# First convolution block's low weight parts by VectorE, S2 formed second, head 0's cached keys requested as attention opens, merge steps later

## The chip, the cores and the metric

The kernel runs on one core of one Trainium2 chip. Its time is the device time of one execution in microseconds (us), as the median of several runs. TensorE (PE) multiplies, VectorE (DVE), ScalarE (ACT) and GpSimd (POOL) do the element-wise work, and the queue of SyncE (SP) issues most of the transfers; POOL issues those that accumulate. Each engine takes its instructions in the order in which the program emits them.

## What is computed

One inference step of a decoder trunk with four layers, for 512 prompt tokens and 8 sample tokens that share every weight. The token mixers are an mLSTM matrix memory (layer 0), a gated short convolution (1), a dilated windowed attention (2) and a causal pooling (3); each layer ends with a gated per-layer embedding. What the change touches, cut from the reference:

```python
x += mixer(rms_norm(x, norm_g[i]))
x = x + sigmoid(x @ pg_w[i]) * (p[i] @ pe_w[i])

# layer 1
bg, cg, xb, z = split(h @ w_in, 4)            # w_in is the kernel's w_b
cx = cg * xb
y = conv_w[0] * cpad[:, 0:T] + conv_w[1] * cpad[:, 1:1+T] + conv_w[2] * cpad[:, 2:2+T]
out = (bg * y * silu(z)) @ w_out

# layer 2, three dilation groups per head: softmax statistics of each group, then
mx = max over groups of m
num = sum over groups of l * exp(m - mx) * o ;  den = sum of l * exp(m - mx)
```

For the sample tokens the keys and values of attention come from a cache (`kc0` to `kc2`, `vc0` to `vc2`).

## The kernel before

**Products.** All matrices are float32. Each weight tile (128x1024, 512 KB) and each activation is split into a high part and a low part in the reduced format fp32r, and a product is three matmuls: high by high, high by low, low by high (`mm6`, L334 to L338). A projection over 1024 inputs is 48 matmuls on 256 or 264 columns. Its sum lies in one of two PSUM buffers (`ps`), which is drained by DVE or ACT into an `a` tile before the projection after the next may begin.

**Weights.** `plan` lists the weight tiles in the order of use, one `Item` for a single tile and one for a pair. `due` gives each step on an item a planned time: load (SP, L270), high part (ACT, L253), low part. The low part is DVE's subtraction weight minus high part (L262), or, for items marked `moved`, ACT writes minus the high part (L258) and POOL issues a transfer that adds the weight onto it (L260). Before, all tiles of `w_b` and `w_bo` are moved; of a pair only the first. `pump` emits the steps that are due whenever PE's program has moved on. There are four buffers each of loaded weights (`wf`) and of high and low parts (`wh`, `wl`).

**Convolution layer.** The first three channel blocks (`NPLAIN`) are four single projections each, with the tiles 32+j, 16+j, j, 48+j of `w_b`. The norm of the layer's input runs beside the first block: PE adds the squares (L533), ACT takes the root (L534), DVE the reciprocal (L536), and only then can the first projections be drained, by a multiplication with that reciprocal (L485). After that the norm's generator `summed` forms sums of the activations on POOL (L582 to L585) and splits them on ACT and DVE (L589 to L602). From block 3 on, two tiles at a time go through `seven`, a Strassen-like form with seven products of 12 matmuls each: `r1` collects products 1 and 4, and ACT copies `r1` (L377) between them. It needs sums of the two tiles, made by POOL in the step `sum` (S1, the difference in place of the second tile, S2, S4: L277 to L280), then split by ACT into `hs` and by DVE into `ls` at the times given in `due`. The last product of a pair is kept back (`pend`) and emitted after the fourth product of the next pair (`flush`), followed by what the block does with its result (L1109, L1071, L1076 to L1079).

**Streams.** Between the projections' matmuls generators are advanced: one tick after every second `mm6`, so four ticks in a projection. In the mLSTM and in attention `main` (the prompt's work of a head) takes one step a tick; in attention `samp` (the sample tokens' work) takes 1.15. A `yield` ends a step. Head `hd`'s generators start when its projections are done, and so run beside those of head `hd+1`.

**mLSTM head.** `mlstm_head` scales `num` on DVE (L961), yields four times, and has PE transpose it (L967).

**Attention head.** `attn_head` adds the masks (L1238 to L1259), reduces and exponentiates (L1233), bounces the statistics through memory (L1251, L1252), takes the maximum over groups and subtracts it (L1276 to L1278, DVE), exponentiates that (L1279, ACT), scales the probabilities (L1281 to L1292, DVE), waits six steps and transposes them (L1300, PE). `attn_sample_steps` waits two steps, has PE transpose the queries (L1390), sends them to memory (L1393), fetches them back broadcast (`qb`, L1364) and the cached keys (`kc`, L1366), waits six steps and takes dot products on DVE (`sum_k`, L459). At attention's opening SP loads the rotary tables (L1162) and the mask (L1164).

Of the kernel before, what the change touches and what calls it, by code (L numbers as in the profile page):

```python
# [8 lines left out]
F32 = mybir.dt.float32  # L9
# [5 lines left out]
P = 128  # L15
NP = 512
NS = 8
# [25 lines left out]
MOVED = ("w_b", "w_bo")  # L43


class Item:


    def __init__(self, *keys, cost=5.76, life=None):
        self.keys, self.cost, self.life = keys, cost, life  # L50
        self.moved = keys[0][0] in MOVED


def paired(j):
# [58 lines left out]
def due(items):  # L113

    ops, t, seq = [], 0.0, 0
    slots = {"wf": [0.0] * FBUFS, "wh": [0.0] * HBUFS, "hs": [0.0] * SBUFS}

    def take(tag, until):
        free = slots[tag]
        at = min(free)  # L120
        free.remove(at)
        free.append(until)
        return at

    def at(time, i, op):
        nonlocal seq
        ops.append((time, seq, i, op))
        seq += 1
        return time

    for i, it in enumerate(items):
        it.begin = t
        if len(it.keys) == 1:
            ld = min(slots["wf"])
            sp = at(max(ld, take("wh", t + (it.life or it.cost))), i, "split")
            at(take("wf", sp + 3) - 0.01, i, "load")
        else:
            ld, ld2 = sorted(slots["wf"])[:2]
            one = at(max(ld, ld2, t - 12.8), i, "sum")
            h1 = at(max(ld, take("wh", t + 5.76), t - 14.4), i, "high")  # L140
            h2 = at(max(ld2, take("wh", t + 10.08), one + 6.6), i, "high2")
            low1 = at(h1 + 1.3 if it.moved else max(h1 + 1.3, one + 3), i, "low")
            low2 = at(max(h2 + 1.3, one + 3), i, "low2")
            at(take("wf", max(low1, one + 7) + 1) - 0.01, i, "load")
            at(take("wf", low2 + 3) - 0.01, i, "load2")
            for n, need, until in (("2", t - 4.6, t + 2.88), ("1", t - 3.4, t + 4.32), ("4", t - 1.4, t + 17.3)):
                h = at(max(take("hs", until), need, one + 3), i, "high" + "s" + n)
                at(h + 0.6, i, "lows" + n)
        t += it.cost
    return sorted(ops)  # L150
# [42 lines left out]
class Net:  # L193
# [47 lines left out]
    def make(self, i, op):  # L241

        if (i, op) in self.made:
            return
        self.made.add((i, op))
        nc, it = self.nc, self.items[i]
        t = self.wt.setdefault(i, {})
        f = lambda tile: tile.bitcast(F32)
        new = lambda tag, n=1024, pool=None, dt=F32R: (pool or self.wp).tile([P, n], dt, tag=tag, name=self.nm(tag))

        def high(k, tag, n=1024, pool=None):
            t["h" + k] = new(tag, n, pool)
            nc.scalar.activation(t["h" + k], t["w" + k], AF.Copy)  # L253

        def low(k, tag, n=1024, pool=None):
            t["l" + k] = new(tag, n, pool)
            if k == "1" and it.moved:
                nc.scalar.activation(t["l1"], f(t["h1"]), AF.Copy, scale=-1.0)  # L258
                key = it.keys[0]
                nc.gpsimd.dma_start(t["l1"], self.d[key[0]][key[1:]], accum_op=ALU.add)  # L260
                return
            nc.vector.tensor_sub(t["l" + k], t["w" + k], f(t["h" + k]))  # L262

        a, b = slice(0, 512), slice(512, 1024)
        sub = nc.gpsimd.tensor_sub
        if op in ("load", "load2"):
            n = 2 if op == "load2" else 1
            key = it.keys[n - 1]
            t[f"w{n}"] = self.wp.tile([P, 1024], F32, tag="wf", name=self.nm("wf"), bufs=FBUFS)
            nc.sync.dma_start(t[f"w{n}"], self.d[key[0]][key[1:]])  # L270
        elif op == "split":
            high("1", "wh")
            low("1", "wl")
        elif op == "sum":
            w1, w2 = t["w1"], t["w2"]
            s1, s2, s4 = (self.act()[:, :512] for _ in range(3))
            nc.gpsimd.tensor_add(s1, w2[:, a], w2[:, b])  # L277
            sub(w2[:, a], w1[:, a], w2[:, a])
            sub(s2, s1, w1[:, a])
            sub(s4, w1[:, b], s2)  # L280
            t.update(ws1=s1, ws2=s2, ws4=s4)
        else:
            k = op.removeprefix("high").removeprefix("low") or "1"
            step = high if op.startswith("high") else low
            if k[0] == "s":
                step(k, op[0] + "s", 512, self.sp)
            else:
                step(k, "w" + op[0])
# [590 lines left out]
    def mlstm_head(self, hd, q, k, v, so, rows, S):  # L879
        nc, d, m2 = self.nc, self.d, S["m2"]  # L880
# [78 lines left out]
        nc.vector.reciprocal(ss, ss)  # L959
        nc.vector.tensor_mul(ri, ri, ss)  # L960
        nc.vector.tensor_mul(num[:, :, :256], num[:, :, :256], ri.unsqueeze(2).broadcast_to([P, 4, 256]))  # L961
        for _ in range(4):
            yield
        for u in range(2):
            hp = self.aux()
# [186 lines left out]
    def attention(self, h, lay):  # L1152
        nc, d, tc = self.nc, self.d, self.tc
        rope, main, samp = Stream(1), Stream(1), Stream(1.15)
        self.streams = [self.norm, rope, main, samp, self.gate]
        o, self.o_done = [], []
        with ExitStack() as st:
            mp = lay.enter_context(tc.tile_pool(name="at", bufs=1))
            m2 = lay.enter_context(tc.tile_pool(name="at2", bufs=2))
            cs = [self.act()[:32] for _ in range(4)]  # L1160
            for i in range(4):
                nc.sync.dma_start(cs[i], d["rope"][:, i])  # L1162
            mask = mp.tile([P, 512], F32, name="mask")
            nc.sync.dma_start(mask, d["mask"])  # L1164
            for hd in range(H):
                q, k, v = [], [], []
                for g in range(3):
                    keep = 0 if g else NP - P
                    out, tab = (self.by_residue, cs[2:]) if g else (self.scaled, cs[:2])
                    q.append(out(self.proj("w_c", 24 * g + hd, a=h)))  # L1170
                    rope.gens.append(self.rope(q[g], tab))
                    k.append(out(self.proj("w_c", 24 * g + 8 + hd, a=h)))
                    rope.gens.append(self.rope(k[g], tab, d[f"o_k{g}"][hd], keep))
                    v.append(out(self.proj("w_c", 24 * g + 16 + hd, a=h)))
                    nc.sync.dma_start(d[f"o_v{g}"][hd], v[g][:, keep:T])
                rope.drain()
                o.append(self.act())
                main.gens.append(self.attn_head(q, k, v, o[hd], m2, mask))
                samp.gens.append(self.attn_sample(hd, q, k, v, o[hd], m2))
            y, zs = [], []  # L1180

            sent = []

            def gate():
                while len(sent) < min(len(zs), len(self.o_done)):
                    n = len(sent)
                    sent.append(n)
                    self.gated(y, zs[n], o[n], False)

            for j in range(H):  # L1190
                zs.append(self.scaled(self.proj("w_c", 72 + j, a=h)))
                if j > 1:
                    gate()

        def finish():
            main.drain()
            samp.drain()
            gate()

        self.finish = finish  # L1200
        return y
# [13 lines left out]
    def attn_head(self, q, k, v, o, m2, mask):  # L1215
        nc = self.nc
# [47 lines left out]
        for g in range(3):  # L1264
# [3 lines left out]
            t = self.act()  # L1268
# [7 lines left out]
        nc.vector.tensor_max(ma, m3[:, 0], m3[:, 1])  # L1276
        nc.vector.tensor_max(ma, ma, m3[:, 2])
        nc.vector.tensor_sub(m3, m3, ma.unsqueeze(1).broadcast_to([P, 3, 4]))  # L1278
        nc.scalar.activation(mx, mx, AF.Exp)  # L1279
        yield  # L1280
        nc.vector.tensor_mul(l, l, mx)  # L1281
# [3 lines left out]
        f = m2.tile([P, 12], F32, tag="f", name=self.nm("f"))  # L1285
# [41 lines left out]
        for n, i in enumerate(order):  # L1327
            g, c, cols = uses[i]
# [3 lines left out]
        nc.vector.tensor_copy(o[:, :NP], op)  # L1332
        yield

    def attn_sample(self, hd, q, k, v, o, m2):
        nc, d = self.nc, self.d
        mm = nc.tensor.matmul
        qs = m2.tile([P, 3, NS], F32, tag="qs", name=self.nm("qs"))
# [2 lines left out]
        for g in range(3):  # L1341
# [5 lines left out]
            nc.gpsimd.tensor_copy(two(qs[:, g]), new(q[g]))  # L1347
            nc.gpsimd.tensor_mul(two(qk[:, g]), new(q[g]), new(k[g]))
            nc.gpsimd.tensor_copy(two(vn[:, :, g]), new(v[g]))
        return self.attn_sample_steps(hd, qs, qk, vn, o, m2)  # L1350

    def attn_sample_steps(self, hd, qs, qk, vn, o, m2):
        nc, d = self.nc, self.d
        mm = nc.tensor.matmul
        off = (0, 128, 256)
        wait = lambda n: range(n)
# [4 lines left out]
        def load_k(g):  # L1361
            n = NROWS[g]
            qb.append(m2.tile([P, NS, P], F32, tag="qb", name=self.nm("qb")))
            nc.sync.dma_start(qb[g][:n], scr[g].partition_broadcast(n))  # L1364
            kc.append(m2.tile([P, NS, P], F32, tag="kc", name=self.nm("kc")))
            nc.sync.dma_start(kc[g][:n], d[f"kc{g}"][hd])  # L1366

# [17 lines left out]
                if b % 4 == 3:  # L1385
                    yield

        yield from wait(2)
        qp = self.aux()
        nc.tensor.transpose(qp[:24, :P], qs.rearrange("p a b -> p (a b)"), self.ident)  # L1390
        qt = m2.tile([24, P], F32, tag="qt", name=self.nm("qt"))
# [287 lines left out]
```

## Time and profile before

| | us |
|---|---|
| median of 3 runs | 2178.26 |
| lowest and highest | 2176.53, 2182.1 |
| the profiled execution, its own time | 2174.19 |
| its span in the trace | 2172.4 |

| engine | busy us | share of the span |
|---|---|---|
| PE | 2134.1 | 98% |
| DVE | 1393.8 | 64% |
| ACT | 901.0 | 41% |
| POOL | 415.1 | 19% |

The span is what the trace shows of the program; the execution's own time has 1.8 us more around it. An engine's "idle before" is the time it stood still just ahead of an instruction, and the name behind the arrow is what ended that wait. PEclk is TensorE's granted clock, 1.00 for 2.4 GHz and 0.50 for 1.2 GHz.

### The profile page before, as it was taken

The page shows a single profiled execution, that of the slowest core. Times are in us where ns is not written, and L with a number is a line of the kernel's source. Part 1 is how long each engine was busy: PE and PEld are TensorE (multiplying, and loading weights), DVE is VectorE, ACT ScalarE, POOL GpSimd, SP SyncE. Part 2 cuts the span into 40 slices and gives each one's busy share as a digit, 9 for nine tenths or more (in the row PEclk, how much of TensorE's full clock was granted, in tenths as well). Part 3 has the DMA queues.
Part 4 walks back from the last instruction along what each step waited for, and adds up shares of the span by engine and source line. Part 5 has one row for each costly group of instructions (what it writes and reads, how often), then busy time and mean ns, then how long its engine had stood idle before and what let it go on. Part 6 is the DMA issues. An engine that isn't in the chain of part 4 may idle for free.

```text
span 2172.4 us, 42676 instructions
## 1 busy us (share of the span) xinstructions
PE 2134.1 (98%) x17560; PEld 2112.8 (97%) x17560; DVE 1393.8 (64%) x3060; ACT 901.0 (41%) x1438; POOL 415.1 (19%) x491
## 2 busy tenths in 40 slices
PE   8999999999999999999999999999999999999998
PEld 8999999999999999999998999999999999999998
DVE  7676667653466766751477787787876566676434
ACT  6444454432465554554333333333335342322233
POOL 1101110100035545521014332232320000000000
PEclk9999999999999999999999999999999999999999
DMA  5644454332277666687233555455555233223421
GB/s 165 207 159 139 155 183 159 99 106 90 86 170 165 156 175 156 154 200 184 88 118 121 191 174 178 158 190 167 184 165 185 88 113 101 88 90 96 127 79 50
DMA packets 113527, 307.32 MB, mean 141 GB/s; under 512 B 34324, under 2 KB 38676, under 8 KB 111284
## 3 DMA queue, kind: packets, MB, share of 16 engines
q1 hardware_dynamic: 104404, 272.54, 38.2%
q0 software_dynamic: 8784, 31.99, 8.5%
q8 instruction: 138, 2.26, 0.4%
q14 instruction: 57, 0.47, 0.1%
q10 hardware_dynamic: 144, 0.06, 0.0%
HBM read 281.72 MB, written 22.82 MB: 140 GB/s over the span
## 4 chain that ended last, share of the span: by engine, by line
PE 80%; DVE 9%; issue 3%; ACT 3%; DMA 3%; POOL 1%; SPq 0%; DVEq 0%; ACTq 0%; POOLq 0%
PE ps L334 21%; PE ps L336 21%; PE ps L338 21%; PE ax L364 1%; DVE wl L262 1%; PE ax L362 1%; PE ax L363 1%; PE ax L334 1%; PE ax L338 1%; PE ax L336 1%; PE ps L362 1%; PE ps L363 1%; PE ps L364 1%; PE ax L1329 1%; DMA kc<-kc 1%
## 5 line engine op out<-in xcount | busy, mean ns | idle before, releaser
L334 PE MATMUL ps<-hi,wh 128*128 128x256 f32 x4672 | 964.0, 288 | 11.1 <-DVE a L485 7.1
L336 PE MATMUL ps<-lo,wh 128*128 128x256 f32 x4672 | 941.7, 283 | 1.0 <-DVE lo L800 0.8
L338 PE MATMUL ps<-hi,wl 128*128 128x256 f32 x4672 | 941.5, 283 | 0.6 <-DMA wl<-w_bo 0.4
L334 PEld LDWEIGHTS ps<-hi,wh 128*128 128x128 f32 x4672 | 727.2, 189 | 17.7 <-issue 7.4
L336 PEld LDWEIGHTS ps<-lo,wh 128*128 128x128 f32 x4672 | 725.9, 189 | 1.4 <-DVE lo L800 1.0
L338 PEld LDWEIGHTS ps<-hi,wl 128*128 128x128 f32 x4672 | 725.5, 189 | 1.0 <-DMA wl<-w_bo 0.6
L262 DVE TENSOR_TENSOR wl<-wf,wh 128x1024 fp32r<-128x1024 f32 x283 | 356.6, 1263 | 179.0 <-ACT wh L253 176.5
L253 ACT ACTIVATE wh<-wf 128x1024 fp32r<-128x1024 f32 x344 | 361.0, 1053 | 162.2 <-issue 86.3
L1207 POOL TENSOR_TENSOR a<-a,a 32x520 f32<-32x520 f32 x48 | 74.4, 1551 | 273.5 <-DVE a L485 101.8
L502 ACT ACTIVATE a<-ps 128x520 f32<-128x520 f32 x42 | 47.6, 1133 | 133.4 <-PE ps L338 112.2
L260 POOL DMA_DIRECT2D wl<-w_b x45 | 39.8, 884 | 327.4 <-ACT wl L258 308.1
L627 DVE TENSOR_TENSOR x<-ps,x 128x520 f32<-128x520 f32 x32 | 22.4, 699 | 122.8 <-PE ps L338 122.7
L1208 POOL TENSOR_TENSOR a<-a,a 32x520 f32<-32x520 f32 x48 | 66.3, 1382 | 144.6 <-DVE a L1206 98.5
L489 ACT ACTIVATE a<-a 128x520 f32<-128x520 f32 x42 | 26.8, 639 | 147.2 <-DVE a L485 147.1
L466 ACT ACTIVATE hi<-x 128x520 fp32r<-128x520 f32 x32 | 20.5, 639 | 156.9 <-DVE x L627 156.9
L485 DVE TENSOR_TENSOR a<-ps,a 128x520 f32<-128x520 f32 x85 | 59.0, 694 | 21.2 <-PE ps L338 17.8
L649 DVE TENSOR_TENSOR a<-ax,a 128x256 f32<-128x256 f32 (+1 forms) x62 | 23.7, 424 | 75.3 <-ACT a L647 75.3
L459 DVE CUSTOM_DVE_ANT_0 kc<-kc,qb 128x128 f32<-128x128 f32 (+1 forms) x192 | 58.0, 356 | 20.7 <-DMA kc<-kc 20.7
L1233 ACT ACTIVATE S<-S,nmx 128x128 f32<-128x128 f32 (+1 forms) x96 | 39.9, 417 | 72.3 <-DVE nmx L1230 72.3
L258 ACT ACTIVATE wl<-wh 128x1024 fp32r<-128x1024 f32 x61 | 64.6, 1058 | 1.6
L459 DVE CUSTOM_DVE_ANT_0 vc<-vc,pb 128x128 f32<-128x128 f32 (+1 forms) x192 | 61.8, 379 | 1.8 <-DMA pb<-scr_p 1.3
L262 DVE TENSOR_TENSOR ls<-a,hs 128x512 fp32r<-128x512 f32 x57 | 62.6, 1128 | 0.0
(344 smaller groups left out, 2890.5 us busy)
## 6 DMA issues: line engine op xcount, KB each, us to landing
wf<-w_c SPq DMA_DIRECT2D x80, 512.0 KB, 5.6
wf<-w_a SPq DMA_DIRECT2D x64, 512.0 KB, 3.7
wf<-w_b SPq DMA_DIRECT2D x64, 512.0 KB, 3.6
wl<-w_b POOLq DMA_DIRECT2D x45, 512.0 KB, 6.4
wf<-w_pg SPq DMA_DIRECT2D x32, 512.0 KB, 3.6
wf<-w_d SPq DMA_DIRECT2D x32, 512.0 KB, 3.4
pb<-scr_p SPq DMA_DIRECT2D x8, 1292.0 KB, 6.5
Ci<-C_in SPq DMA_DIRECT2D x16, 512.0 KB, 7.5
```

What stands on the lines that cost most here:

```text
L253: nc.scalar.activation(t["h" + k], t["w" + k], AF.Copy)
L258: nc.scalar.activation(t["l1"], f(t["h1"]), AF.Copy, scale=-1.0)
L262: nc.vector.tensor_sub(t["l" + k], t["w" + k], f(t["h" + k]))
L334: mm(out[j], wh, a[0][:, PARTS[j]], start=start, stop=False)
L336: mm(out[j], wh, a[1][:, PARTS[j]], start=False, stop=False)
L338: mm(out[j], wl, a[0][:, PARTS[j]], start=False, stop=stop)
L362: mm(out, w[0][:, c], hi, start=start and k == 0, stop=False, **go)
L459: self.nc.vector.tensor_tensor_reduce(junk, a, b, 1.0, 0.0, ALU.mult, ALU.add, out)
L485: nc.vector.tensor_mul(dst[:, :T], ps, self.r)
L502: nc.scalar.activation(dst, split(ps), AF.Copy)
L1207: nc.gpsimd.tensor_mul(b[:32], t[:32], cs[0])
L1208: nc.gpsimd.tensor_mul(a[:32], a[:32], cs[1])
```

## The change

Five edits. The tiles 0, 16, 32 and 48 of `w_b` (first block) are no longer moved, so DVE makes their low parts. In the pairs POOL forms S2 ahead of the difference that replaces the second tile, and the splits of S2, S1 and S4 are due 2.2, 1.4 and 0.6 us earlier. In mLSTM's head 0 the transposes come two ticks later. In attention the keys `kc0` and `kc1` of head 0 are requested at the opening, into the two buffers of that tag, and head 0's `samp` waits four steps instead of two. In every attention head one `yield` stands between L1278 and L1279.

```diff
-        self.moved = keys[0][0] in MOVED
+        name, j = keys[0][:2]
+        self.moved = name in MOVED and not (name == "w_b" and j % 16 == 0)
...
-            for n, need, until in (("2", t - 4.6, t + 2.88), ("1", t - 3.4, t + 4.32), ("4", t - 1.4, t + 17.3)):
+            for n, need, until in (("2", t - 6.8, t + 2.88), ("1", t - 4.8, t + 4.32), ("4", t - 2.0, t + 17.3)):
...
             nc.gpsimd.tensor_add(s1, w2[:, a], w2[:, b])
+            sub(s2, s1, w1[:, a])
             sub(w2[:, a], w1[:, a], w2[:, a])
-            sub(s2, s1, w1[:, a])
             sub(s4, w1[:, b], s2)
...
         nc.vector.tensor_mul(num[:, :, :256], num[:, :, :256], ri.unsqueeze(2).broadcast_to([P, 4, 256]))
-        for _ in range(4):
+        for _ in range(4 if hd else 6):
             yield
...
             nc.sync.dma_start(mask, d["mask"])
+            early = []
+            for g in range(2):
+                early.append(m2.tile([P, NS, P], F32, tag="kc", name=self.nm("kc")))
+                nc.sync.dma_start(early[g], d[f"kc{g}"][0])
...
         nc.vector.tensor_sub(m3, m3, ma.unsqueeze(1).broadcast_to([P, 3, 4]))
+        yield
         nc.scalar.activation(mx, mx, AF.Exp)
...
             nc.sync.dma_start(qb[g][:n], scr[g].partition_broadcast(n))
+            if early:
+                kc.append(early.pop(0))
+                return
             kc.append(m2.tile([P, NS, P], F32, tag="kc", name=self.nm("kc")))
             nc.sync.dma_start(kc[g][:n], d[f"kc{g}"][hd])
...
-        yield from wait(2)
+        yield from wait(2 if hd else 4)
```

## Rows read from the trace of the kernel before

**Rows 1.** The page's section 1: busy us, share and instructions of each engine.
```profile
PE 2134.1 (98%) x17560; PEld 2112.8 (97%) x17560; DVE 1393.8 (64%) x3060; ACT 901.0 (41%) x1438; POOL 415.1 (19%) x491
```

**Rows 2.** PE's waits: line waited for, us in total, times, longest.
```profile
PE ps L334 <- DVE a L485: 7.1, 4, 3.0
...
PE ax L364 <- DVE ls L262: 3.2, 6, 0.6
PE ps L334 <- ACT a L478: 2.5, 2, 2.2
PE ax L967 <- ACT Ci L998: 2.0, 1, 2.0
PE ax L1390 <- POOL qs L1347: 1.8, 1, 1.8
PE ax L1300 <- DVE S L1292: 1.7, 3, 0.6
```

**Rows 3.** Stretches: busy us (instructions) of PE, PEld, DVE, ACT, POOL; PEclk, DMA, GB/s.
```profile
550.00:600.00 50.00, 50.00 (x419) 50.00 (x419) 26.12 (x39) 20.64 (x29) 1.04 (x1) 1.00 0.29 90
...
1190.64:1194.05 3.41, 3.41 (x18) 3.41 (x17) 3.41 (x13) 0.00 (x0) 3.41 (x2) 0.50 0.13 54
1388.61:1392.02 3.41, 2.90 (x14) 2.60 (x14) 3.24 (x13) 2.36 (x3) 1.83 (x1) 0.50 0.95 250
```

**Rows 4.** Timeline at mLSTM head 0's transposes: start, us, instruction, [idle before].
```profile
101.42 1.23 DVE L961 TENSOR_TENSOR num<-num,ri 128x1024 f32<-128x1024 f32 x1
...
102.79 1.06 PE L967 MATMUL ax<-ident,num 128*128 128x128 f32 x8 [2.04 <-ACT Ci L998]
```

**Rows 5.** Timeline of ACT and PE beside the first convolution block.
```profile
609.28 1.06 ACT L258 ACTIVATE wl<-wh 128x1024 fp32r<-128x1024 f32 x1
...
610.40 1.04 PE L533 MATMUL ax<-a,onesd 128*128 128x256 f32 x4
...
613.69 0.84 ACT L534 ACTIVATE a<-ax,eps 128x256 f32<-128x256 f32 x2
```

**Rows 6.** Timeline of DVE beside the first convolution block.
```profile
614.20 3.41 DVE L536 RECIPROCAL a<-a 128x256 f32<-128x256 f32 x2 [5.02 <-ACT a L534]
617.72 0.70 DVE L485 TENSOR_TENSOR a<-ps,a 128x520 f32<-128x520 f32 x1
...
624.46 4.55 DVE L593 TENSOR_TENSOR lo<-a,hi 128x520 fp32r<-128x520 f32 x2 [3.36 <-ACT hi L589]
...
630.77 0.69 DVE L485 TENSOR_TENSOR a<-ps,a 128x520 f32<-128x520 f32 x1
```

**Rows 7.** Timeline of a pair that follows a pair (six such), POOL, ACT and DVE.
```profile
713.01 1.63 POOL L278 TENSOR_TENSOR wf<-wf,wf 128x512 f32<-128x512 f32 x1
714.61 1.31 POOL L279 TENSOR_TENSOR a<-a,wf 128x512 f32<-128x512 f32 x1
...
714.68 1.06 ACT L253 ACTIVATE wh<-wf 128x1024 fp32r<-128x1024 f32 x1 [2.96 <-POOL wf L278]
...
724.51 0.37 ACT L377 ACTIVATE a<-ax 128x260 f32<-128x260 f32 x1
...
717.54 1.17 DVE L1109 TENSOR_TENSOR a<-a,a 128x520 f32<-128x520 f32 x1
...
721.36 0.69 DVE L262 TENSOR_TENSOR ls<-a,hs 128x512 fp32r<-128x512 f32 x1
```

**Rows 8.** Timeline of SP as attention opens, of SP and DVE before head 0's dot products.
```profile
1110.23 0.37 SPq L1164 DMA_DIRECT2D mask<-mask  x1
1115.14 1.46 SPq L270 DMA_DIRECT2D wf<-w_c  x2
...
1182.51 0.32 SPq L1364 DMA_DIRECT2D qb<-scr_q  x1
...
1184.09 0.67 DVE L1269 COPY a<-ax 128x512 f32<-128x512 f32 x1
1188.26 0.29 DVE L459 CUSTOM_DVE_ANT_0 kc<-kc,qb 128x128 f32<-128x128 f32 x1 [3.50 <-DMA kc<-kc]
```

**Rows 9.** Timeline of ACT ahead of the wait that precedes the second clock drop.
```profile
1387.45 0.21 ACT L1279 ACTIVATE st<-st 128x12 f32<-128x12 f32 x1 [9.43 <-DVE st L1278]
```

More of the change, by code (lines that the diff above doesn't have):

```diff
@@ L1178, in attention @@
                 main.gens.append(self.attn_head(q, k, v, o[hd], m2, mask))
-                samp.gens.append(self.attn_sample(hd, q, k, v, o[hd], m2))
+                samp.gens.append(self.attn_sample(hd, q, k, v, o[hd], m2, early))
             y, zs = [], []
@@ L1333, in attn_head, with attn_sample @@
         yield
-    def attn_sample(self, hd, q, k, v, o, m2):
+    def attn_sample(self, hd, q, k, v, o, m2, early):
         nc, d = self.nc, self.d
@@ L1349, in attn_sample, with attn_sample_steps @@
             nc.gpsimd.tensor_copy(two(vn[:, :, g]), new(v[g]))
-        return self.attn_sample_steps(hd, qs, qk, vn, o, m2)
-    def attn_sample_steps(self, hd, qs, qk, vn, o, m2):
+        return self.attn_sample_steps(hd, qs, qk, vn, o, m2, early)
+    def attn_sample_steps(self, hd, qs, qk, vn, o, m2, early):
         nc, d = self.nc, self.d
```

## The prediction

> **What bounds the kernel now.** The first view is the table of engines: PE is busy for 98% of the span and the next engine for 64% [rows 1]. So time can be won only where PE stands still or runs slowly. The second view is the list of PE's waits. Its six lines that bear on this change hold 18.3 us (7.1 + 3.2 + 2.5 + 2.0 + 1.8 + 1.7) [rows 2]. The third is the table of stretches. Undisturbed, PE starts 419 matmuls in 50 us, 0.119 us each, so a tick of 12 is 1.43 us and a projection 5.7 us. Twice, behind the longest L485 wait and behind the long L478 wait, the granted clock is 0.50 (1.2 GHz) for 3.41 us, and only 18 and 14 matmuls start [rows 3], where 28.6 fit. The 18 are worth 2.1 us of work, a loss of 1.3; half of 3.41 is 1.7; I take 1.5 for such a drop. Last I read the timelines around each wait, for who is late and what stands in his queue.
>
> **mLSTM, head 0.** PE's transposes L967 waited 2.04 us for the scaling L961, which ran from 101.42 to 102.65 [rows 4]. (The row names an ACT line, which had long been done; L967 reads what L961 writes.) PE was there at 102.79 - 2.04 = 100.75. Two ticks later is 103.6, behind 102.65, so the wait goes: **2.0 us**. The two yields stay in `main`: head 1 begins two ticks later, head 2 also a little, and head 3 on time, since a head needs 19 of 24 ticks. No row shows heads 1 and 2 at that offset. The nearest row for what an offset can do is this wait itself, so I bound it by 2.0 either way and take 0.
>
> **First convolution block.** On ACT the block's low parts stand between its high parts and the norm's root L534; one is at 609.28, 1.06 us long, and another such follows before the root at 613.69. DVE idles 5.02 us for that root [rows 5, 6]. Without the two the root starts at 613.69 - 2.1 = 611.6, and PE's sums L533 that it reads are done at 611.44 [rows 5]. The reciprocals, and the drain L485 that stood at 617.72, move by 2.1 too. Behind this, everything up to the second late drain at 630.77 is a chain of DVE, POOL and ACT steps (L593 with 4.55 us is its largest) in which nothing waits for PE [rows 6]. It and its continuation move together, so PE gains the chain's shift, **2.1 us**, out of the 4.1 of the three shorter L485 waits (7.1 - 3.0) [rows 2]; the rest of these waits stays. Bounds: 0, if the drain is late for another reason, to 4.1. The four subtractions that DVE takes over cost about 1.4 us each, an estimate from 0.69 for half the columns [rows 7]. Two fall into the 5.02 us idle, the other two beside the embedding, where DVE has no drain due; taken at nothing. Without that cover each would delay a drain by 1.4. The `wf` buffers come free 1.4 us later, but four loads stand between a release and its use. POOL loses four transfer issues.
>
> **Pairs.** Six times, where a pair follows a pair, PE waits 0.53 us on average (3.2 / 6) for `ls` of S2 [rows 2]. That subtraction started at 721.36 because it stood on DVE behind the flushed block's work (L1109 to L1079) [rows 7]. Its due time is now t - 6.2, not t - 4.0. The flush comes after the pump at t - 4.32, so it moves ahead of the flush and the wait goes. What is late next is ACT's copy L377, which ended at 724.88 [rows 7]. From the wait's end at 722.05, PE has 22 matmuls (2.6 us) to the fourth product, which adds to `r1` and so needs that copy: 724.7. PE is thus already at that limit, and 0.53 earlier it must wait unless L377 is earlier. One split of 0.5 us (S1) moves from between L1071 and L377 into ACT's idle time ahead of the flush. Against it, the high part at 714.68 waits for POOL's difference L278 [rows 7], which is now third, behind S2 (1.31 us). DVE's low part stands behind that high part, L1109 behind that, and L1071 waits for L1109. POOL's sequence starts some 0.5 earlier, since the accumulating transfer ahead of it waits for one ACT split less, and L1109 (1.17 [rows 7]) would be nearer 0.7 if POOL has finished by then. I take 0.13 left per pair: 6 x 0.4 = **2.4 us**, with bounds 3.2 and -0.6 (L377 later by 0.1 than now, 6 times).
>
> **Attention opens.** SP is free from 1110.6 to 1115.14 [rows 8], so the two early requests of 0.4 us pass nothing. Their 1 MB beside the next weight load costs nothing I can see: queries and keys, 2 MB, landed within 5.75 us of 1182.51 [rows 8], so 1 MB is done by about 1115. L1390 waited 1.8 us for POOL's copies [rows 2]; two `samp` steps later it doesn't: **1.8**. The longest L485 wait (3.0) is a drain behind four dot products, which themselves waited 3.50 us for the keys [rows 2, 8]. By the rate of 1.15, `sum_k` was step 9 in tick 8, the last of its projection and so ahead of that projection's drain. With four waits it is step 11 in tick 10, behind it. Then the drain follows L1269, which ends at 1184.76 [rows 8], and is done at 1185.5. PE wanted it at 1189.8 - 3.0 = 1186.8, now 1.8 earlier at 1185.0. About 0.6 of the wait remains: **2.4**. DVE reaches the dot products near 1188.5, when the queries alone are due no later than 1188.26 as before. With the wait short, the clock drop behind it goes: **1.5**. Bounds of the three: 1.8, if the drain is late anyway, and 6.3.
>
> **Merge.** All of `main` behind L1278 comes a tick (1.43) later, the scaling L1292 and the transposes L1300 alike. But L1292 stood behind DVE's backlog, so it gains time on L1300, except for one `samp` step of four dot products (about 0.9) that may now come first. 1.43 - 0.9 just covers the 0.57 of each of three waits [rows 2]: **1.7**, bounds 0 and 1.7. It does nothing for the L478 wait and the second drop. L1279, which held ACT for 9.43 us [rows 9], moves from tick 10 to 11, and the drain L478 behind it is emitted after tick 12. I take 0 there; 4.0 if it went (2.5 + 1.5).
>
> **Sum.** 2.0 + 2.1 + 2.4 + (1.8 + 2.4 + 1.5) + 1.7 = 13.9, say 14 us: the profiled 2174.2 becomes 2160. The median shown is 4.1 above that execution, and I carry that over: 2178.3 - 14 = **2164**. With all gains at their upper ends it is 2.0 + 4.1 + 3.2 + 6.3 + 1.7 + 4.0 = 21 and 2157; with the pairs, the opening and the merge at their lower ends, 2.0 + 2.1 - 0.6 + 1.8 + 0 = 5 and 2173.
>
> **Rivals.** *The wait moves to L377.* For it: the copy is already at the limit. Against it: ACT gets rid of a split there. Price: the 2.4 of the pairs, and with the same backlog on DVE in head 0 the merge's 1.7 and 1 more: 2164 + 5 = 2169. The Trainium skill ("SBUF — State Buffer", Who interferes with whom) says that a VectorE instruction with two SBUF inputs and a GpSimd one that reads SBUF exclude each other for whole instructions, the first to issue winning. The trace agrees: two L593 took 4.55 us [rows 6] beside POOL's sums. By that rule the moved `ls`, now beside POOL's sums, would be stretched too, and this rival is the one that it speaks for.
>
> *The opening stays as it is.* The queries alone hold the dot products, or the drain is late for another reason; then only the 1.8 comes there, 3.9 less: 2168, and 2173 with the first rival. For it: SP issues the queries at 1182.51 only because it waits for an earlier bounce, and that stays. Against it: the drain no longer stands behind them.
>
> *Slower: the clock falls in each pair.* If S2's earlier split on ACT, which waits for POOL, holds ACT so long that PE waits 2.5 us or more for L377, as long as the wait ahead of the second drop [rows 2, 3], each of six pairs costs 2.5 + 1.5 in place of 0.53. That is 24.0 - 3.2 = 20.8 worse than now, against 11.5 won elsewhere: 2178.3 + 9.3 = 2188. It decides at 2.5 us, and waits of 2.0 and 1.8 (L967, L1390) had no drop behind them. The chain above gives 0.1 to 0.6, so the chance is small.
>
> **How the numbers follow.** Forecast 0.58 (2164, own range 2158 to 2170); first rival 0.20; second 0.16; slower 0.06. Within 0.3% (6.5 us, about what a measurement of this kernel can tell from no change) is 2171.8 to 2184.8. Faster: nearly all of the forecast (0.56), most of the first rival (0.15), about half of the second (0.09): 0.80. Slower: 0.06. The same: 0.14. The range 2157 to 2174.5 leaves out the slow rival and the tails.
>
> **What would show it.** Right: no PE wait on L967, L1390 or `ls`, the root near 611.6, a drain near 1185 ahead of the dot products, and one clock drop, not two. Wrong: PE waits on L377 of 0.5 us or more, the first convolution block's drains unmoved, the clock at 0.50 near 1186, or new waits in mLSTM heads 1 and 2.

## The result and the profile after

The changed kernel takes 2164.7 us (median of 4 runs, 2164.1 to 2165.6) where the kernel before, run beside it, takes 2177.7 (median of 4, 2176.5 to 2182.1): a ratio of 0.9944 with a 95% interval of 0.993 to 0.9959, faster by 9 to 15 us. The forecast was 2164.0 with a range of 2157.0 to 2174.5.

The sum of the forecast is another matter. The profiled execution after takes 2164.99 us. That is 9.2 us less than the profiled one before (2174.19), not 13.9, and the terms do not stand as forecast. PE's waits in the trace after, as line waited for, us in total, times, longest (the edits move lines down by 1 to 9: L485 is L486 here, L1300 is L1306):

```profile
PE ps L335 <- ACT a L1542: 5.2, 1, 5.2
PE ax L363 <- ACT a L378: 5.0, 6, 0.8
PE ax L1306 <- DVE S L1298: 4.2, 4, 2.0
PE ps L335 <- DVE a L486: 1.5, 2, 0.8
PE ax L1272 <- DVE qt L1401: 1.2, 1, 1.2
...
PE ax L968 <- DVE num L962: 0.3, 1, 0.3
```

Beside [rows 2]: L1390, the long drain L485 and L478 are gone, L967 (now L968) is down from 2.0 to 0.3, and the shorter drains from 4.1 to 1.5 (0.8 of it in the convolution blocks, the rest in the mLSTM). But six waits on the copy L377 (now L378) stand where six on `ls` stood, 5.0 us for 3.2; L1300 (now L1306) rose from 1.7 in three waits to 4.2 in four; and L1272 <- L1401 is new. The first line has its like in the kernel before (5.1 us, near the end) and no part in this.

To see where time went I matched the projections' matmuls of two traces by their order (those that write `ps`, 14804 in each) and took how much earlier or later the same matmul starts. The differences over four stretches, one execution each, against the profiled execution of before:

| kernel | mLSTM, 73 to 348 us | conv blocks 0 to 2, 605 to 674 | pairs, 674 to 950 | attention, 1150 to 1641 | whole |
|---|---|---|---|---|---|
| before, a second execution | +4.9 | 0.0 | 0.0 | +5.0 | +10.0 |
| changed | -0.6 | -3.6 | +1.7 | -6.2 | -9.4 |

The second execution of the same kernel is 10 us slower than the first. So the first question was what the executions of the kernel before differ in; the second was what the five edits do one by one.

### The profile page after: what moved, and what is told of

It is laid out like the page before. It is cut to its first block, busy times and chain, and to the rows that moved or that the text cites. A ratio compares the mean times of both kernels' runs of the same rounds, so it can differ in the third digit from the quotient of the medians.

```text
span 2163.2 us, 42666 instructions
## 1 busy us (share of the span) xinstructions
PE 2131.4 (99%) x17560; PEld 2111.3 (98%) x17560; DVE 1388.3 (64%) x3064; ACT 899.8 (42%) x1434; POOL 406.6 (19%) x487
## 4 chain that ended last, share of the span: by engine, by line
PE 76%; DVE 9%; DMA 5%; issue 4%; ACT 4%; POOL 2%; SPq 0%; ACTq 0%; DVEq 0%; POOLq 0%
PE ps L335 21%; PE ps L339 20%; PE ps L337 20%; DVE wl L263 2%; ACT wh L254 1%; PE ax L337 1%; PE ax L339 1%; PE ax L335 1%; PE ax L363 1%; PE ax L365 1%; PE ax L1335 1%; PE ax L364 1%; DMA kc<-kc 1%; DVE kc L460 1%; DMA wl<-w_b 1%
## 5 line engine op out<-in xcount | busy, mean ns | idle before, releaser
L263 DVE TENSOR_TENSOR wl<-wf,wh 128x1024 fp32r<-128x1024 f32 x287 | 363.4, 1270 | 159.4 <-ACT wh L254 156.8
L486 DVE TENSOR_TENSOR a<-ps,a 128x520 f32<-128x520 f32 x85 | 58.9, 692 | 21.0 <-PE ps L339 17.6
```

The lines of the kernel that those rows point to most:

```text
L486: nc.vector.tensor_mul(dst[:, :T], ps, self.r)
```

## The experiments

Times are medians; those of the kernel before, run beside them on the same chip, stand in the next column. They lie between 2171.7 and 2177.7, so kernels that were not run beside each other are better compared by their ratios.

| kernel | us | before beside it | ratio, 95% interval |
|---|---|---|---|
| changed | 2164.7 | 2177.7 | 0.9944, 0.993 to 0.9959 |
| b_again | 2177.2 | 2176.6 | 1.0002, 0.9991 to 1.0013 |
| u_pairs | 2164.8 | 2176.6 | 0.9951, 0.9939 to 0.9963 |
| u_merge | 2169.8 | 2176.6 | 0.9975, 0.9964 to 0.9985 |
| f_split | 2162.5 | 2176.6 | 0.9933, 0.9921 to 0.9946 |
| ac_only | 2168.8 | 2176.7 | 0.9966, 0.9953 to 0.9978 |
| d_only | 2176.4 | 2176.7 | 1.0004, 0.9995 to 1.0013 |
| k_only | 2173.8 | 2176.7 | 0.9988, 0.9979 to 0.9996 |
| e_only | 2178.2 | 2176.7 | 1.0002, 0.9994 to 1.0011 |
| f2_split | 2156.1 | 2174.5 | 0.9912, 0.9898 to 0.9927 |
| f3_turn | 2151.6 | 2174.5 | 0.9891, 0.9875 to 0.9908 |
| f2_nopair | 2161.7 | 2171.7 | 0.9954, 0.9941 to 0.9966 |
| f4_wait3 | 2152.8 | 2171.7 | 0.9908, 0.9894 to 0.9921 |

The same table of stretches for them, one profiled execution each, against the first of before:

| kernel | mLSTM | conv blocks 0 to 2 | pairs | attention | whole |
|---|---|---|---|---|---|
| ac_only | -3.1 | -3.7 | 0.0 | +0.2 | -6.5 |
| d_only | +0.4 | +0.1 | +0.5 | +0.7 | +1.5 |
| k_only | +2.4 | 0.0 | 0.0 | +0.5 | +4.0 |
| e_only | +0.7 | +0.1 | 0.0 | +1.2 | +3.9 |
| u_merge | -3.0 | -3.6 | +2.8 | -0.8 | -5.0 |
| u_pairs | -2.4 | -3.7 | +0.1 | -2.0 | -7.9 |
| f_split | -0.9 | -3.7 | -1.7 | -3.6 | -11.4 |
| f2_split | -3.5 | -3.6 | -5.6 | -4.4 | -18.5 |
| f2_nopair | -1.4 | -3.7 | -1.1 | -4.7 | -11.0 |
| f3_turn | -2.7 | -3.7 | -5.6 | -10.1 | -23.3 |
| f4_wait3 | -3.2 | -3.7 | -5.6 | -11.0 | -24.3 |

### b_again: the kernel before, once more

No edit.

> The kernel before, unchanged. Theory: its executions differ by what the two drops of the granted clock and the landing times of the queries and keys cost, so another profiled execution shows other L478 and L485 waits than 2.2 and 3.0 us, or another number of stretches at 0.50, and a span that differs from 2172.4 us by these waits. Rival: the trace is the same but for noise, within 1 us in each wait, and the difference between the profiled execution (2174.19) and the median (2178) does not lie in the waits.

Its profiled execution took 2184.3 us. The stretches of its trace, with columns as in [rows 3]; PEclk is the third number from the end:

```profile
102.00:106.00 4.00, 3.39 (x19) 3.42 (x20) 4.00 (x9) 0.56 (x2) 0.00 (x0) 0.66 0.41 156
...
204.00:208.00 4.00, 2.96 (x9) 2.31 (x10) 3.79 (x12) 0.00 (x0) 0.83 (x2) 0.71 0.48 133
1190.00:1200.00 10.00, 5.58 (x32) 5.41 (x32) 5.50 (x22) 0.28 (x1) 3.81 (x2) 0.78 0.63 231
...
1390.00:1400.00 10.00, 6.98 (x54) 6.45 (x53) 9.76 (x46) 3.52 (x5) 3.33 (x2) 0.85 0.62 200
```

The clock fell four times and not twice: behind L967's wait (102 to 106 us), L943's (204 to 208), L485's (1190 on) and L478's (1390 on). The first two drops last 3.41 us each, the other two 6.83 (1195.57 to 1202.40 and 1396.95 to 1403.78, both at 0.50). Its PE waits:

```profile
PE ps L334 <- DVE a L485: 8.5, 4, 4.4
...
PE ax L943 <- DVE C L931: 2.9, 3, 2.0
PE ps L334 <- ACT a L478: 2.8, 3, 2.1
...
PE ax L967 <- ACT Ci L998: 2.0, 1, 2.0
```

L967's wait is 2.0 us here as in the first execution [rows 2, 4], yet here the clock fell behind it, and the matmuls behind it start 1.5 us later against the first execution: that is what one drop of 3.41 us costs. The theory holds: executions of the kernel before differ by the number and the length of their drops and by a few waits (L943 2.0 for 1.0, L485 4.4 for 3.0). They spread from 2170.5 to 2184.3 us over all runs; the four of the changed kernel lie within 1.5 us.

### ac_only: the two edits that lie by themselves

```diff
+        self.moved = name in MOVED and not (name == "w_b" and j % 16 == 0)
...
+        for _ in range(4 if hd else 6):
```

> The kernel before with two of the five edits, which lie in stretches of their own: the first convolution block's low parts by DVE, and mLSTM head 0's transposes two ticks later. Theory from the trace after: L967's 2.0 us fall to 0.3 or less and no clock drop can follow them; the three shorter L485 waits fall from 4.1 us to 1.5 and the first from 1.4 to nothing, so that the block gains 3.7 us and not the 2.1 of the prediction. In all 5.5 us against before, in an execution whose attention is like the first one's (about 2171). The prediction's terms: 2.0 + 2.1 = 4.1 us.

2168.8 us, 7.9 less than before beside it, of the 13 that the whole change brings. In its trace the first blocks gain 3.7 us, as in each of the nine kernels that have the edit, and mLSTM 3.1: the L967 wait, and the wait of 1.0 us on L943 at 201 us, which is not there. I had expected 5.5.

### d_only and k_only: the opening of attention

d_only has the early keys and the later sample work, k_only the early keys alone.

```diff
+                nc.sync.dma_start(early[g], d[f"kc{g}"][0])
...
-        yield from wait(2)
+        yield from wait(2 if hd else 4)      # d_only, not k_only
```

> The kernel before with the opening's edit alone: keys of head 0 requested early and its sample work two steps later. The prediction's terms: L1390's wait (1.8), 2.4 of the long L485 wait and the clock drop behind it go, 5.7 us in all (about 2171). Theory from the kernel without the merge yield: the same three go, but PE's transposes wait 1.2 us behind the copy of the queries (L1401), and SP issues the third group's queries and keys behind the merge's bounce, so that PE waits 4 us for the last dot products with a clock drop behind; net within 1.5 us of before.

> The kernel before with head 0's first two groups of keys requested early, and no later sample steps. Theory A (the prediction's step: the drain's place behind the dot products is what costs): L1390 keeps 1.8 us and the long L485 wait keeps at least 2 us, with its clock drop; within 1.5 us of before. Theory B (the keys' landing is what costs): the dot products start 1.5 us earlier or more, the L485 wait falls below 1.5 us and its clock drop goes; 3 us faster.

d_only brings nothing: 2176.4 for 2176.7. PE's waits at the opening in d_only, then in k_only:

```profile
PE ax L1417 <- DVE sT L459: 4.1, 1, 4.1
PE ax L1271 <- DVE qt L1399: 1.3, 1, 1.3
```

```profile
PE ax L1397 <- POOL qs L1351: 2.0, 1, 2.0
PE ps L334 <- DVE a L485: 1.9, 1, 1.9
```

In d_only the waits of 1.8 and 3.0 are gone, as the prediction had it, and 1.3 and 4.1 stand in their place, with a clock drop behind the 4.1. That is the theory from the kernel without the merge yield (u_merge, below). In k_only the dot products wait 2.50 us for the queries where they waited 3.50 for the keys [rows 8], so the keys' landing was worth 1 us and the queries hold the rest. Neither theory has its number (1.9, between "at least 2" and "below 1.5"); the drop stays, so theory A is the nearer. It gains 2.9 us, 1 to 4.6 by its interval, which its single trace does not show.

### e_only and u_merge: the merge's yield, alone and taken out

```diff
         nc.vector.tensor_sub(m3, m3, ma.unsqueeze(1).broadcast_to([P, 3, 4]))
-        yield            # u_merge: taken out of the changed kernel; e_only: put into the kernel before
         nc.scalar.activation(mx, mx, AF.Exp)
```

> The kernel before with the merge's extra yield alone. The prediction's term: the three L1300 waits of 0.57 us go, 1.7 us. Theory from the trace after: further dot products and a sum of the normalisation come ahead of the scaling on DVE, so the waits stay at 0.5 to 0.9 us each: within 1 us of before. On the L478 wait: if it depends on when the queries' write lands (2.9 us in one execution, 1.2 in another) it stays at 0.4 to 2.2 us; if the yield cures it, none above 0.5 us is left.

> The changed kernel without the yield ahead of the merge's exponential. Theory from the trace after: that yield lets further sample dot products in ahead of the merge's scaling on DVE, so that it gained nothing; without it head 0's wait for the scaled probabilities falls from 2.0 us to 0.6 or less, those of heads 1 to 3 from 0.6, 0.9 and 0.6 to 0.57 each, and the time by 1.5 to 2.5 us (2162.2 to 2163.2). The prediction's step: the yield gains 1.7, so 2166.4. A rival on the long L478 wait: if this yield had removed it, it returns here with a clock drop, 4.0 us more (2168.7); if not, no drop shows.

Alone the yield brings nothing (2178.2 for 2176.7, ratio 1.0002), and the L1300 waits rise from 1.7 to 4.2. Taken out of the changed kernel it costs 5.1 us (6.7 by the ratios), at least three times what the prediction gave it and against my expectation from the trace after. The rival that I named is a small part of it: the L478 wait is back with 1.4 us, but without a clock drop. SP at the opening in the changed kernel, and then in u_merge (there with a row of DVE and one of PE that wait):

```profile
1188.88 0.55 SPq L1370 DMA_DIRECT2D qb<-scr_q  x1
1189.48 0.58 SPq L1375 DMA_DIRECT2D kc<-kc  x1
...
1192.33 0.33 SPq L1295 DMA_DIRECT2D scr_f<-f  x1
```

```profile
1188.26 0.33 SPq L1294 DMA_DIRECT2D scr_f<-f  x1
1190.00 0.38 SPq L1295 DMA_DIRECT2D f<-scr_f  x1
1191.46 0.55 SPq L1369 DMA_DIRECT2D qb<-scr_q  x1
1192.06 0.58 SPq L1374 DMA_DIRECT2D kc<-kc  x1
...
1196.56 0.28 DVE L460 CUSTOM_DVE_ANT_0 kc<-kc,qb 64x128 f32<-64x128 f32 x1 [1.68 <-DMA kc<-kc]
...
1202.49 0.27 PE L1418 MATMUL ax<-ident,sT 64*8 64x64 f32 x1 [4.00 <-DVE sT L460]
```

The merge's scaling is followed by a bounce of `f` through memory, two transfers on SP, the second of which waits for the first. The third group's queries and keys are requested by `samp` on the same queue. Two sample steps later (the opening's edit), these requests fall behind the bounce: issued at 1191.46, 3.2 us later than in the changed kernel if both are counted from PE's transposes L1272 (1177.34 here, 1178.01 there). DVE then waits for the keys, PE waits 4.0 us for the dot products, and the clock falls. With the yield the bounce is a tick later and the requests go first. So neither edit gains by itself, and the two together gain 2.0 to 6.2 us in attention (the five kernels that have both and no edit at L1300: changed, u_pairs, f_split, f2_split, f2_nopair).

The yield does a second thing. Queries of head 2, SP in ac_only (no yield) and in e_only (yield):

```profile
1365.79 0.33 SPq L1398 DMA_DIRECT2D scr_q<-qt  x1
1369.38 0.33 SPq L1366 DMA_DIRECT2D qb<-scr_q  x1
```

```profile
1376.10 0.31 SPq L1398 DMA_DIRECT2D scr_q<-qt  x1
1378.13 0.34 SPq L1366 DMA_DIRECT2D qb<-scr_q  x1
```

From the issue of the queries' write to that of the read that waits for it, the six traces without the yield (two of before, ac_only, d_only, k_only, u_merge) have 2.9 to 3.7 us, and head 2's L478 waits 1.4 to 2.5. The eight with it have 1.3 to 2.0, and the wait is at most 0.5, but for 1.3 in e_only. So in these traces, one of each kernel, the wait is shorter with the yield, if narrowly in e_only (1.3, against 1.4 in u_merge). Why the write is done sooner I could not read from the traces; it stays open.

### u_pairs, f_split, f2_split and f2_nopair: the pairs

u_pairs is the changed kernel with the pair edit undone (order on POOL and due times).

> The changed kernel with the pair edit undone (POOL's order and the due times of the splits of S2, S1 and S4 as before). Theory from the trace after: the six waits on ACT's copy L378 (5.0 us in all) go, six waits of 0.53 us on ls of S2 (3.2) return, and the kernel is faster by 1.8 us than the changed one (2164.7 to 2162.9). The prediction's step held that the edit gains 2.4 us, so undoing it would give 2167.1.

The time is the same, 2164.8 for 2164.7 (ratios 0.9951 and 0.9944), not 1.8 us less. In its trace the pairs are as before (+0.1, the six `ls` waits are back) where the changed kernel has +1.7, so the edit loses there as the theory says. In this one execution attention takes the gain away again, with a clock drop near 1192 and 6.6 us of L1306 waits; that the median is held up by the same is not shown.

The pair at 710 us in the changed kernel, POOL, then ACT, then DVE, beside [rows 7]:

```profile
706.49 1.58 POOL L278 TENSOR_TENSOR a<-wf 128x512 f32<-128x512 f32 x1
708.15 1.64 POOL L279 TENSOR_TENSOR a<-a,wf 128x512 f32<-128x512 f32 x1
709.75 1.29 POOL L280 TENSOR_TENSOR wf<-wf,wf 128x512 f32<-128x512 f32 x1
711.00 1.74 POOL L281 TENSOR_TENSOR a<-wf,a 128x512 f32<-128x512 f32 x1
...
711.07 1.06 ACT L254 ACTIVATE wh<-wf 128x1024 fp32r<-128x1024 f32 x1 [0.61 <-POOL wf L280]
...
714.92 0.73 ACT L1072 ACTIVATE a<-a,cols 128x520 f32<-128x520 f32 x1 [2.00 <-DVE a L1110]
715.56 1.05 ACT L254 ACTIVATE wh<-wf 128x1024 fp32r<-128x1024 f32 x1
716.63 1.06 ACT L259 ACTIVATE wl<-wh 128x1024 fp32r<-128x1024 f32 x1
717.60 0.61 ACT L254 ACTIVATE hs<-a 128x512 fp32r<-128x512 f32 x1
718.12 1.05 ACT L254 ACTIVATE wh<-wf 128x1024 fp32r<-128x1024 f32 x1
719.20 1.06 ACT L259 ACTIVATE wl<-wh 128x1024 fp32r<-128x1024 f32 x1
720.16 0.37 ACT L378 ACTIVATE a<-ax 128x260 f32<-128x260 f32 x1
...
712.16 1.65 DVE L263 TENSOR_TENSOR wl<-wf,wh 128x1024 fp32r<-128x1024 f32 x1 [0.58 <-ACT wh L254]
713.74 0.41 DVE L373 TENSOR_TENSOR a<-ps,a 128x260 f32<-128x260 f32 x1
714.19 0.70 DVE L1110 TENSOR_TENSOR a<-a,a 128x520 f32<-128x520 f32 x1
```

From L1072 on ACT does not rest until the copy is done. Two splits stand there that need not. That from 715.56 could run while ACT idles 2.00 us ahead of L1072, but is emitted behind the flush. That from 718.12 is due exactly at the pair's begin and so emitted just ahead of the copy, for a tile that the plan wants 16 us later. f_split moves the second, f2_split both:

```diff
+            w = it.keys[0][0] == "w_b" and it.keys[0][1] % 16 >= NPLAIN
+            late = (0.8 if it.keys[0][1] >= 48 else -0.05) if w else 0.0     # f_split: 0.8 for both
-            sp = at(max(ld, take("wh", t + (it.life or it.cost))), i, "split")
+            sp = at(max(ld, take("wh", t + (it.life or it.cost))) + late, i, "split")
```

> The changed kernel with one more edit: the splits of the single tiles of w_b behind the first three blocks are due 0.8 us later, so that the one due exactly at a pair's begin is emitted behind ACT's copy L378 and not ahead of it. Theory: that split (1.05 and 1.06 us on ACT) is what keeps the copy late; the copy ends near 718.4 where it ended at 720.53, PE's six waits of 0.83 us go, and the time falls by up to 5.0 us to 2159.7. Rival: something next to it (S4's split, DVE's low parts) is late by nearly as much, and less than 2 us is won.

> The changed kernel with the split that is due at a pair's begin emitted behind the copy L378 (0.8 us later, as before), and the split of the other single tile emitted ahead of the flushed block's work and not behind it (0.05 us earlier). In the kernel with the first of these alone the copy's waits went, and PE waited 3.1 us in three places for a low part that POOL's accumulating transfer brings; that transfer's first step on ACT (wh) started 1.8 us after the product that frees its buffer, because ACT stood idle ahead of L1072. Theory: it starts some 1.5 to 2 us earlier, these three waits go, and L378 waits stay away: 3 us faster than that kernel (2162.5 to 2159.5). Rival: ahead of L1072 the split delays the flushed block, and with it the copy or ls, and what is won is lost there.

> The kernel f2_split (ACT's queue ahead of the copy L378 cleared) with the pair edit undone: POOL's order and the due times of S2, S1 and S4 as before the change. Theory: the pair edit does take the ls wait away, and its gain was hidden by the copy that was late next; with the copy out of the way, undoing it brings six waits of 0.53 us on ls back, 3.2 us (2156.1 to 2159.3). Rival: the cleared queue alone is enough and the pair edit is idle; no ls wait shows, the time stays within 1 us.

PE's waits from 700 to 960 us in f_split and in f2_nopair; f2_split has none at all there:

```profile
PE ps L340 <- DMA wl<-w_b: 3.1, 3, 1.2
```

```profile
PE ax L367 <- DVE ls L265: 3.2, 6, 0.6
```

f_split removes all six waits on the copy, and meets the next one: three waits for low parts that come by transfer. It gains 2.2 us and not 5. f2_split removes these too: 2156.1 us, 8.5 less than the changed kernel (7.0 by the ratios), and 7.3 less in the pairs (+1.7 to -5.6). f2_nopair, the same without the pair edit, has the six `ls` waits again and 4.6 us more in the pairs (-1.1 for -5.6), where I had expected 3.2; its median, not measured beside f2_split's, is 5.6 higher. So the pair edit does what it says. By these traces it is worth 4.6 us once ACT's queue is clear, and costs 1.7 while it isn't.

### f3_turn and f4_wait3: more ticks and fewer

```diff
-        for _ in range(6):       # steps between the merge's scaling and the transposes L1300
+        for _ in range(7):
...
-        yield from wait(2 if hd else 4)
+        yield from wait(2 if hd else 3)      # f4_wait3 alone
```

> The kernel f2_split with seven instead of six steps between the merge's scaling and its transposes L1300. Theory: the scaling's place on DVE does not change, PE comes a tick (1.43 us) later, so the waits there fall from 2.0 and 1.5 each to 0.6 and 0.1, 4.2 to 5.9 us less in all, and a clock drop behind head 0's becomes impossible. Rival: a later step of the head (the products with the values, or the sample part that follows) has no such tick to spare and waits in place of it; less than 1.5 us is won.

> The kernel f3_turn with head 0's sample work one step later instead of two (three steps of waiting, not four). Theory: the copy of the queries L1401 comes ahead of DVE's next low part, so PE's 1.2 us on the transposes that wait for its buffer go, L1399 waits 0.4 us or less for POOL's copies, the drain stays ahead of the dot products, and the last dot products come a tick earlier, so that of the 2.0 us that PE waits for them 0.6 is left: 2 to 2.5 us faster than f3_turn (2151.6 to 2149.3). Rival: the dot products are one tick nearer to the drain and go ahead of it, the L485 wait of 3.0 us returns with its clock drop, 3 us slower.

f3_turn takes 2151.6 us, 4.5 less than f2_split beside it and 13 less than the changed kernel (11.5 by the ratios); it is the fastest kernel here (ratio 0.9891, 0.9875 to 0.9908). Its waits from 1160 to 1560 us:

```profile
PE ax L1421 <- DVE sT L462: 2.0, 1, 2.0
PE ax L1274 <- DVE qt L1403: 1.2, 1, 1.2
PE ax L1308 <- DVE S L1300: 0.2, 1, 0.2
```

6.1 us of f2_split's waits at the transposes fell to 0.2, and the rival has its part: one wait of 2.0 for the last dot products is new. The clock drop behind head 0's wait in f2_split (1184 us) is gone with it. Waits and drop together make 6.1 - 0.2 - 2.0 + 1.5 = 5.4 us, and the attention stretch of the table has 5.7. In f4_wait3 both upper lines are gone as expected, and 0.7, 0.7 and 0.5 came elsewhere (L481, L1308 twice); the long drain wait of the rival did not return. Its trace is 1.0 us shorter than f3_turn's, its median 1.2 longer, but not measured beside it: no difference that these runs can tell.

## Why the prediction was right, and where it was not

The time and the range were right; the sum behind them came out right by luck, by misses that cancel. Term by term, forecast and measured:

**mLSTM: 2.0, measured about 4.** L967's wait went, but for 0.3:

```profile
102.83 1.23 DVE L962 TENSOR_TENSOR num<-num,ri 128x1024 f32<-128x1024 f32 x1
...
140.48 1.06 PE L968 MATMUL ax<-ident,num 128*128 128x128 f32 x8 [0.30 <-DVE num L962]
```

That 0.3 is head 1's. What was mis-sized is all around it. The offset of the next heads was taken at 0; with it a wait of 0.9 to 2.0 on L943 near 202 us, in all five traces without the edit, is gone in seven of nine (1.1 is left in f_split and f2_nopair). And that the wait of 2.0 "had no drop behind" it was the luck of one execution. Over the table the nine kernels with the edit average -2.3 us in mLSTM, the five traces without it +1.7.

**First convolution block: 2.1, measured 3.65** (from -3.64 to -3.66 in nine traces). The mechanism is as forecast. ACT, then DVE, in the changed kernel, beside [rows 5, 6]:

```profile
610.68 0.85 ACT L535 ACTIVATE a<-ax,eps 128x256 f32<-128x256 f32 x2
...
614.70 0.70 DVE L486 TENSOR_TENSOR a<-ps,a 128x520 f32<-128x520 f32 x1
...
627.73 0.69 DVE L486 TENSOR_TENSOR a<-ps,a 128x520 f32<-128x520 f32 x1
...
640.85 2.39 DVE L594 TENSOR_TENSOR lo<-a,hi 128x520 fp32r<-128x520 f32 x2
...
651.01 0.69 DVE L486 TENSOR_TENSOR a<-ps,a 128x520 f32<-128x520 f32 x1
```

The root came 3.0 us earlier, of which 0.85 was won upstream: 2.15. The two drains moved by the same, 3.0 each. The rest, 1.5, is a term that the sum lacked. The next pair of L594 took 2.39 us, where the kernel before has

```profile
643.90 3.83 DVE L593 TENSOR_TENSOR lo<-a,hi 128x520 fp32r<-128x520 f32 x2
...
655.51 0.69 DVE L485 TENSOR_TENSOR a<-ps,a 128x520 f32<-128x520 f32 x1
```

The third late drain (the last row of each) came 4.50 us earlier, and less the 0.85 that is the 3.65. In exchange two of POOL's sums beside the pair took 1.28 and 1.21 us for 0.87 and 0.86. The Trainium skill ("SBUF — State Buffer", Who interferes with whom) says that of a VectorE instruction with two SBUF inputs and a GpSimd one that reads SBUF the first to issue goes first and the other waits. That they hold each other up the traces show: an operation of this shape with two inputs takes 0.69 us while POOL is idle (L1083 at 641.22 before), and L593 takes 1.2 to 3.4 beside POOL's sums. The order of issue does not explain what changed: POOL's first sum starts ahead of this pair of L593 in both kernels, by 0.40 us before and by 0.45 in the changed one. Before, three sums end while the first subtraction of the pair stands (2.67 us); in the changed kernel one does (1.21 us). What turned this is not shown. "It and its continuation move together" was the step that failed, to the good side.

**Pairs: 2.4 gained, measured 1.7 lost.** The first rival (chance 0.20) took place, and at a worse price than it was given. The wait moved to L377, as named. The step that failed is "I take 0.13 left per pair". Of what speaks for an earlier copy, L1110 took 0.70 (1.17 before) and one split of 0.5 left ACT, as forecast. What I named and did not price was larger: the difference is third on POOL, so `wh` starts at 711.07, 1.3 us ahead of the end of the product that `flush` waits for (712.4), where it was 2.2 ahead (714.68 and 716.9 in the trace before). DVE's low part behind it then ran beside POOL's last sum (1.65 us for 1.23), and L373 started 1.34 us behind the product and not 0.18. 1.16 lost, 0.99 won: behind that product the copy is 0.15 later. PE comes to it 0.53 earlier and had nothing to spare: in all six such pairs of the kernel before (each the third of three in a row), its first matmul behind the copy already followed the one ahead of it by 0.19 to 0.21 us and not by 0.12. Matched matmul by matmul, each pair wins some 0.79 at `ls` and loses some 0.92 at the copy, 0.7 us in six. Another 0.7 of the 1.7 is not at the copy: two short stops, at 898.7 and 941.9 us, stand where f_split has two of its three waits for low parts that come by transfer.

**Opening, 5.7, and merge, 1.7; measured 4.2 together** (the mean of five traces, 2.0 to 6.2, against the first execution of before; against the mean of the three traces with the attention of before, 0, 5.0 and 0.2 in the tables, it is 5.9), and nothing for either alone. The step on the drain was right: it stands at 1181.40, ahead of the dot products (1187.07), and neither its wait nor the drop behind it is in any trace with the edit. L1390's 1.8 went too, but for a wait of 1.2: two steps later the copy of the queries (L1401) stands behind a low part on DVE, and PE's next transposes want its buffer. The step that failed is the one that stopped at the drain. I followed the moved steps past DVE and not past SP, where the third request fell behind the merge's bounce. The merge's own step was wrong in its mechanism: the extra yield does not bring the scaling ahead of PE (L1306's waits are 4.2 us for 1.7, since twelve dot products, where four were before, and a sum L1216 still come first), it brings the request ahead of the bounce.

**L478's wait and the second drop: 0, measured up to 4.0** (within the 4.2 above). Forecast to stay; the upper end of the range held the 4.0. They went with the yield, as far as the traces tell by way of the queries' write and not of L1279's place on ACT, which I had looked at: that line still holds ACT ahead of the drain, for 7.50 us in the changed kernel. The 2.5 is two waits; the one ahead of the drop is 2.2, so the slower rival's "as long as the wait ahead of the second drop" was read from the wrong number.

**The 4.1 us between the profiled execution and the median.** Carried over as a constant, it stood in effect for drops and waits that differ between executions: the kernel before had two drops in that execution, four in another. The changed kernel has none while PE still works, and its profiled execution lies on its median (2164.99 and 2164.7). So the forecast of 2160 for that execution was 5 us too low, and that of the median was right because the 4.1 disappeared: mLSTM and the first blocks gave 3.5 us more than forecast, pairs and attention 7.3 less. That leaves 10.1 of the 13.9, near the 9.2 between the two executions; with the 5.9 for attention it would be 11.8, so this sum is good to a few us only.

## What to carry to other kernels

Follow a moved step on every queue that it issues to, and name what it now stands behind: here a request behind a bounce on SP turned 5.7 us into nothing, and one tick on another stream gave it back. Where PE already touches the next limit behind the one that you remove, remove both or expect to lose: the pair edit cost 1.7 us, and gained 4.6 when two due times were moved as well. A short wait of PE may be followed by a clock drop in one execution and not in the next, so a kernel's median can lie several us from the trace that you read.

## What was not expected of the hardware

- Waits of 2.0 to 2.1 us of PE were followed by the clock at half speed in some executions (L967 in b_again and k_only, L1306 in u_pairs, f2_split and f2_nopair) and not in others (L967 in before and e_only, L1306 in the changed kernel and f_split). A wait of 2.5 (L478 in ac_only) had none; one of 1.9 (L1395 in ac_only) and one of 1.7 (L478 in k_only) had one. So the 2.5 us at which the slower rival decides is no limit here. While PE works a drop lasts 3.41 or 6.83 us in these traces; one of 3.41 cost 1.5 us.
- A stop of PE cost more than the idle time in the list of waits: 0.77 us for an `ls` wait of 0.53 (the steps between f2_nopair and f2_split, pair by pair) and 1.09 for a copy wait of 0.83 (between the changed kernel and f2_split), some 0.25 more in each.
